# First and last sums of squares of a hybrid decoder block: an early table load, sums by source, single stores

## The chip, the cores and the metric

The kernel runs on one core of one Trainium2 chip. The metric is the device time of one execution in microseconds, and lower is better. The kernel before was timed three times: 1016.0 us in the median, from 1015.67 to 1016.91. Its profile comes from one further execution. The engines are called as the profile calls them: PE (TensorE, matmuls), PEld (its weight loads), DVE (VectorE), ACT (ScalarE), POOL (GpSimd), SP (SyncE, which issues most DMAs).

## The reference, cut to what matters

One decoder layer in float32, with 512 tokens of width 1024: a feed-forward block, a token-mixing block, a second feed-forward block, and a last RMSNorm. Nine vectors made from the condition `c` shift, scale and gate the three blocks.

```
def rmsnorm(x, g):
    y = x * rsqrt(mean(x * x, axis=-1, keepdims=True) + EPS)
    return y * g

cond = silu(c)
sh1, sc1, gt1, ..., sh3, sc3, gt3 = split(cond @ w_ada + b_ada, 9)
u = rmsnorm(h, g_norm_ffn1) * (1 + sc1) + sh1
h = h + 0.5 * gt1 * swiglu(u, w_ffn1_in, w_ffn1_out)
u = rmsnorm(h, g_norm_mix) * (1 + sc2) + sh2
h = h + gt2 * token_mixing(u, ...)
u = rmsnorm(h, g_norm_ffn2) * (1 + sc3) + sh3
h = h + 0.5 * gt3 * swiglu(u, w_ffn2_in, w_ffn2_out)
return rmsnorm(h, g_final)
```

The change touches the sums of squares of the first RMSNorm, those of the last one with the stores behind it, and the helper that also serves the two RMSNorms between.

## The kernel before, in words

**Layout.** The activations are kept transposed: `H[k]`, k = 0 to 7, is 128 features by 512 tokens. Tokens lie along the free axis, so a mean over features is a sum over partitions and over the eight tiles. Squares are taken on ACT, the eight tiles are added up (mostly on DVE, into `acc`), and PE sums over partitions with a matmul against a tile of ones. Half A is tokens 0 to 255, half Bh tokens 256 to 511.

**Matmuls.** A weight is split into a high and a low part (ACT writes `whi`, L298, DVE writes `wlo`, L310), the activations likewise, and each product is three matmuls (`mm3`, L341 to L343). Plain float32 matmuls, such as the sums, the fillers and the spreads, show two records each in the profile.

**The order of the work.** It is written out by hand: each engine runs its instructions in the order in which the Python code issues them, and so does each DMA queue (SP's, and near the end ACT's). No scheduler moves anything. Semaphores are put in where one engine needs another's result or buffer.

**The head (`startup`).** PE first runs five filler matmuls (`warm`, L1411). SP loads `c` (one row), the eight tiles of `H`, then the first tiles of `wada`, small vectors (`vecs`, `cst`) and the first weights (`raw`). ACT waits for `c`, loads the table for Silu and computes silu(c) into row 0 of a zeroed tile (L1431); two matmuls with ones spread that row over all partitions (L1433). DVE and ACT copy the two halves of the result into `cond` (L1435, L1446; ACT's copy stands between the squares of k = 4 and k = 5). ACT squares the eight tiles of `H` as they land (L1448). DVE adds the squares of k = 0, 2, 4, 6 into `acc` and those of k = 1, 3, 5 into `R` (L1450), then `R` into `acc` (L1454); the square of k = 7 stays alone. Between these PE runs fillers on `H[0]` to `H[5]`, twelve in all, and then the sums from two sources, the square of k = 7 and `acc`, four matmuls each (L1440). The sums come out as 128 equal columns, of which ACT reads one per 128 tokens for the square root (L1458). DVE takes the reciprocal (L1463) between the first two products of `ada_do` (L364, rows of `wada` times `cond`), PE spreads it over the partitions with an identity matrix (L1466), and DVE and ACT make the first normalized tile `UH` (L444, L456). With that the stream of main matmuls starts (L1506, L1508, L1510).

**The helper (`stats_t`, L419 to L432).** For one half it sums over partitions with one matmul per 128 tokens and source, each with a single column of ones, so that the result is one column per 128 tokens. The loop runs over tokens outside and over sources inside. It is called five times beside main matmuls (in `out_tail` and `head`, twice each, and for half A in `out_end`) and once at the very end. `spread` (L434) puts the result back over the partitions, two matmuls of 128 columns for a half.

**The tail (`out_end`).** The last weight matrix is applied in steps m = 3 to 7, first for half A, then for half Bh. After each step DVE adds the gated result to `H[m]` (`tail_step`, L493), ACT squares it into a tile `s` (L494), ACT scales `H[m]` by the last norm's weights into `O[m]` (`scaled`, L545), and DVE adds `s` to `acc` (L580). While half Bh is computed, half A is finished: its sums at the middle of m = 4, its spread at the middle of m = 5, then a multiplication by the spread reciprocal (`final`, L549) of tiles 0 to 3 on POOL, which reads an SBUF copy `R`, and of tiles 4 and 5 (after m = 5) and 6 and 7 (after m = 6) on DVE, which reads the bank. SP stores them in pairs. After m = 7 of half Bh come five fillers (L591), the sums from two sources (`acc` and the last `s`), two more fillers, the spread (L437), and the last eight finals: six on DVE, and tiles 1 and 2 on POOL, for which ACT copies the spread bank into `R` (L601). The stores are (0), (1) and (2) on SP's queue and the pairs (3, 4), (5, 6) and the single (7) on ACT's (L552).

Of the kernel before, what the change touches and what calls it, by code (L numbers as in the profile page):

```python
# [11 lines left out]
AF = mybir.ActivationFunctionType  # L12
OP = mybir.AluOpType

P = 128
T = 512
# [120 lines left out]
class Kernel:  # L137
# [281 lines left out]
    def stats_t(self, bank, hs, parts=None, between=None):  # L419


        n = (hs.stop - hs.start) // P
        r, c = self.r4[:, hs.start // P:hs.stop // P], slice(hs.start, hs.start + n)
        parts = parts or (self.acc[:, hs],)
        for i in range(n):
            for j, x in enumerate(parts):
                self.nc.tensor.matmul(bank[:, hs.start + i:hs.start + i + 1], x[:, i * P:i * P + P], self.ones[:, 0:1],
                                      start=j == 0, stop=j == len(parts) - 1)
        self.nc.scalar.activation(r, bank[:, c], AF.Sqrt, bias=self.eps, scale=1.0 / D)
        if between:  # L430
            between()
        self.nc.vector.reciprocal(r, r)  # L432
# [102 lines left out]
    def out_end(self, ms, ksrc, gate):  # L535

        nc = self.nc
        v, g = nc.vector, nc.gpsimd
        tiles = {}
        A, Bh = slice(0, HT), slice(HT, T)  # L540
        rA, rB = self.B[6], self.B[7]
        self.held = self.pos

        def scaled(m, hs):
            nc.scalar.activation(self.O[m][:, hs], self.H[m][:, hs], AF.Copy, scale=self.g(3)[:, m:m + 1])  # L545

        def final(e, m, hs, r):
            o = self.O[m][:, hs]
            e.tensor_tensor(o, o, r[:, hs], op=OP.mult)  # L549

        def store(m0, m1, hs, queue):
            queue.dma_start(self.out[m0 * P:m1 * P, hs].rearrange("(m p) t -> p m t", p=P), self.OO[:, m0:m1, hs])  # L552

        for h, hs in enumerate((A, Bh)):
            for m in ms:
                bank = self.nb()
                if h == 0:
                    tiles[m] = ksrc(m)
                    self.split_hi()
                    if m == ms[0]:  # L560
                        nc.scalar.preload_act_table(AF.Sqrt)
                n = len(tiles[m])
                for i, (hi, lo, uh, ul) in enumerate(tiles[m]):
                    if h and m == ms[1] and i == n // 2:
                        self.stats_t(rA, A)
                    if h and m == ms[2] and i == n // 2:
                        self.spread(rA, A)
                        nc.scalar.activation(self.R[:, A], rA[:, A], AF.Copy)
                        for j in range(4):
                            final(g, j, A, self.R)  # L570
                            if j % 2:
                                store(j - 1, j + 1, A, nc.sync)
                    self.mm3(bank[:, hs], hi, lo, uh[:, hs], ul[:, hs], i == 0, i == n - 1)
                s = self.tp.tile([P, T], F32, name="ut")[:, :HT]
                self.tail_step(m, hs, bank, gate, s)
                if h and m == ms[-1]:
                    break
                scaled(m, hs)
                self.split_lo()
                v.tensor_tensor(self.acc[:, hs], self.acc[:, hs], s, op=OP.add)  # L580
                if h and m in ms[2:4]:
                    j = 4 + 2 * (m - ms[2])
                    for x in (j, j + 1):
                        final(v, x, A, rA)
                    store(j, j + 2, A, nc.sync)

        free = self.nb()

        def warm(n):
            for _ in range(n):  # L590
                nc.tensor.matmul(free[:, :P], self.ones, self.ones, start=True, stop=True)  # L591

        warm(5)
        self.stats_t(rB, Bh, (self.acc[:, Bh], s))
        warm(2)
        scaled(ms[-1], Bh)
        self.spread(rB, Bh)

        final(v, 0, Bh, rB)
        store(0, 1, Bh, nc.sync)  # L600
        nc.scalar.activation(self.R[:, Bh], rB[:, Bh], AF.Copy)  # L601
        final(g, 1, Bh, self.R)
        for j in (3, 4, 5, 6, 7):
            final(v, j, Bh, rB)
            if j == 4:
                store(3, 5, Bh, nc.scalar)
                store(1, 2, Bh, nc.sync)
                final(g, 2, Bh, self.R)
        store(5, 7, Bh, nc.scalar)
        store(2, 3, Bh, nc.sync)  # L610
        store(7, 8, Bh, nc.scalar)

    def head(self, n, banks, table):

# [789 lines left out]
    def startup(self):  # L1404
        nc, a = self.nc, self.a
        v, M = nc.vector, nc.tensor.matmul


        def warm(n, x):
            for _ in range(n):  # L1410
                M(self.B[5][:, :P], self.ones, x[:, :P], start=True, stop=True)  # L1411

        v.memset(self.ones, 1.0)
        warm(5, self.ones)

# [22 lines left out]
        def part(s, first, last):  # L1438
            for n in range(4):
                M(self.B[7][:, n * P:(n + 1) * P], s[:, n * P:(n + 1) * P], self.ones, start=first and n == 0, stop=last,  # L1440
                  skip_group_check=True)

        acc = (self.acc, self.R)
        for k in range(KT):
            if k == 5:
                nc.scalar.activation(self.cond[:, T:], self.B[1], AF.Copy)  # L1446
            s = acc[k] if k < 2 else self.tp.tile([P, T], F32, name="ut")
            nc.scalar.activation(s, self.H[k], AF.Square)  # L1448
            if 1 < k < 7:
                v.tensor_tensor(acc[k % 2], acc[k % 2], s, op=OP.add)  # L1450
            if k < 6:
                warm((1, 1, 2, 2, 3, 3)[k], self.H[k])
            elif k == 6:
                v.tensor_tensor(acc[0], acc[0], acc[1], op=OP.add)  # L1454
            else:
                part(s, True, False)
                part(acc[0], False, True)
        nc.scalar.activation(self.r4, self.B[7][:, ::P], AF.Sqrt, bias=self.eps, scale=1.0 / D)  # L1458
        warm(2, self.H[7])

        g, b1 = self.g(0), self.vecs[:, 8:16]
# [117 lines left out]
```

## Time and profile before

| what | value |
|---|---|
| runs of the kernel before, median (lowest to highest) | 1016.0 us (1015.67 to 1016.91) |
| the profiled execution's own time | 1016.32 us |
| its span, first to last instruction | 1014.5 us |
| PE busy | 1003.8 us, 99% |
| DVE busy | 764.8 us, 75% |
| ACT busy | 442.0 us, 44% |
| POOL busy | 26.1 us, 3% |
| granted TensorE clock, mean | 0.998 |
| DMA | 139.61 MB, mean 138 GB/s |

Times within a profile count from the start of its span; about 1.8 us of an execution's own time lie outside the span. "Idle" in a row is the time its engine stood before it, with the instruction or DMA that ended the wait. The chain of work follows the last instruction back, at each step to what released it. Records of matmuls overlap, so a matmul's cost in a stream is the distance between starts, not its duration.

### The profile page before, as it was taken

Reading aid. Unit: us, or ns where it says so; the run is one execution under the profiler, and the core shown is the slowest. Engines: PE = TensorE matmul, PEld = TensorE weight load, DVE = VectorE, ACT = ScalarE, POOL = GpSimd, SP = SyncE. Lnnn points to the kernel's source line nnn. Section 1 sums busy time; section 2 is a strip of 40 time slices with the busy share of each in tenths; the row PEclk is TensorE's granted clock in tenths of the full one; section 3 lists DMA queues with packets and bytes.
Section 4 is the critical chain, followed back from the end, with each engine's and each line's share of the span. In section 5 each row is a group of like instructions: output and inputs, shape, how many; then the busy total and the mean of one; then the engine's idle time right before and its main releaser. Section 6 shows DMA issues by size and latency. Waiting matters only on the chain.

```text
span 1014.5 us, 15763 instructions
## 1 busy us (share of the span) xinstructions
PE 1003.8 (99%) x6448; PEld 912.2 (90%) x6448; DVE 764.8 (75%) x1120; ACT 442.0 (44%) x674; POOL 26.1 (3%) x30
## 2 busy tenths in 40 slices
PE   8999999999999999999999999999999999999997
PEld 7888999989899999889988888998899899998997
DVE  7989979789796667878448776577787776676754
ACT  5443644525435443334323333454366254352553
POOL 0000000000000000008000000000000000000001
PEclk9999999999999999999999999999999999999999
DMA  9856456455454323222155773421353234241312
GB/s 336 274 197 214 146 163 221 148 175 168 148 182 136 104 77 104 63 63 84 32 198 188 253 265 107 122 63 62 95 176 122 66 105 146 84 146 43 113 33 83
DMA packets 43114, 139.61 MB, mean 138 GB/s; under 512 B 4897, under 2 KB 8225, under 8 KB 43042
## 3 DMA queue, kind: packets, MB, share of 16 engines
q1 hardware_dynamic: 42354, 137.95, 41.8%
q8 instruction: 50, 0.82, 0.3%
q10 hardware_dynamic: 688, 0.66, 0.2%
q14 instruction: 22, 0.18, 0.1%
HBM read 135.82 MB, written 2.77 MB: 137 GB/s over the span
## 4 chain that ended last, share of the span: by engine, by line
PE 93%; DVE 5%; ACT 1%; issue 1%; DMA 0%; DVEq 0%; ACTq 0%
PE bank L341 16%; PE bank L342 16%; PE bank L343 16%; PE bank L723 10%; PE bank L725 10%; PE bank L724 10%; PE bank L1506 1%; PE bank L1510 1%; PE bank L1508 1%; PE bank L1097 1%; PE bank L1276 1%; DVE wlo L310 1%; PE bank L1277 1%; PE bank L1278 1%; PE bank L1045 1%; PE bank L1074 1%
## 5 line engine op out<-in xcount | busy, mean ns | idle before, releaser
L310 DVE TENSOR_TENSOR wlo<-raw,whi 128x1024 fp32r<-128x1024 f32 (+6 forms) x166 | 174.4, 1062 | 66.5 <-ACT whi L298 65.9
L298 ACT ACTIVATE whi<-raw 128x1024 fp32r<-128x1024 f32 (+6 forms) x166 | 150.0, 920 | 47.6 <-DVE raw L242 41.6
L725 PE MATMUL bank<-UH,wlo 128*128 128x256 f32 x544 | 150.5, 277 | 0.0
L723 PE MATMUL bank<-UH,whi 128*128 128x256 f32 x544 | 150.5, 277 | 0.0
L724 PE MATMUL bank<-UL,whi 128*128 128x256 f32 x544 | 150.5, 277 | 0.0
L341 PE MATMUL bank<-HI,whi 128*128 128x512 f32 (+1 forms) x406 | 146.6, 361 | 0.0
L342 PE MATMUL bank<-HK,whi 128*128 128x512 f32 (+1 forms) x406 | 146.4, 361 | 0.0
L343 PE MATMUL bank<-HI,wlo 128*128 128x512 f32 (+1 forms) x406 | 146.2, 360 | 0.0
L341 PE MATMUL bank<-UH,whi 128*128 128x512 f32 (+1 forms) x400 | 145.9, 365 | 0.0
L343 PE MATMUL bank<-UH,wlo 128*128 128x512 f32 (+1 forms) x400 | 141.8, 355 | 0.5 <-DVE wlo L310 0.5
L342 PE MATMUL bank<-UL,whi 128*128 128x512 f32 (+1 forms) x400 | 141.8, 355 | 0.1
L310 DVE TENSOR_TENSOR wlo<-X,whi 128x1024 fp32r<-128x1024 f32 (+4 forms) x106 | 111.7, 1064 | 33.3 <-ACT whi L298 32.9
L298 ACT ACTIVATE whi<-X 128x1024 fp32r<-128x1024 f32 (+4 forms) x106 | 95.7, 927 | 46.3 <-DVE X L242 45.6
L723 PE MATMUL bank<-SH,whi 128*128 128x256 f32 x408 | 113.8, 279 | 0.1
L724 PE MATMUL bank<-SL,whi 128*128 128x256 f32 x408 | 113.6, 278 | 0.0
L725 PE MATMUL bank<-SH,wlo 128*128 128x256 f32 x408 | 113.6, 278 | 0.0
L724 PEld LDWEIGHTS bank<-UL,whi 128*128 128x128 f32 x544 | 102.3, 188 | 0.3
L723 PEld LDWEIGHTS bank<-UH,whi 128*128 128x128 f32 x544 | 102.1, 188 | 0.3
L725 PEld LDWEIGHTS bank<-UH,wlo 128*128 128x128 f32 x544 | 102.1, 188 | 0.0
L342 PEld LDWEIGHTS bank<-HK,whi 128*128 128x128 f32 x406 | 76.3, 188 | 11.8 <-DVE HK L651 0.4
L341 PEld LDWEIGHTS bank<-HI,whi 128*128 128x128 f32 x406 | 76.5, 188 | 11.5
L343 PEld LDWEIGHTS bank<-HI,wlo 128*128 128x128 f32 x406 | 76.4, 188 | 11.6
(228 smaller groups left out, 1760.2 us busy)
## 6 DMA issues: line engine op xcount, KB each, us to landing
ada<-wada SPq DMA_DIRECT2D x47, 512.0 KB, 5.0
raw<-wmix SPq DMA_DIRECT2D x44, 512.0 KB, 3.6
raw<-wf1i SPq DMA_DIRECT2D x32, 512.0 KB, 4.4
raw<-wf2i SPq DMA_DIRECT2D x30, 512.0 KB, 3.6
X<-wf2i SPq DMA_DIRECT2D x14, 512.0 KB, 3.6
cs<-wada SPq DMA_DIRECT2D x12, 512.0 KB, 3.5
AR<-wada SPq DMA_DIRECT2D x12, 512.0 KB, 4.2
raw<-wf2o SPq DMA_DIRECT2D x12, 512.0 KB, 3.6
```

The costliest lines, as they stand in the source:

```text
L298: self.nc.scalar.activation(self.hi[:, y], r[:, x], AF.Copy)
L310: self.nc.vector.tensor_tensor(self.lo[:, y], r[:, x], self.hi[:, y], op=OP.subtract)
L341: M(ps, hi, uh, start=start, stop=False)
L342: M(ps, hi, ul, start=False, stop=False)
L343: M(ps, lo, uh, start=False, stop=stop)
L723: M(o, hi, uh, start=start and p == 0 and k == 0, stop=False, skip_group_check=True)
L724: M(o, hi, ul, start=False, stop=False, skip_group_check=True)
L725: M(o, lo, uh, start=False, stop=k == 3, skip_group_check=True)
L1045: M(S[:, o + i * P:o + i * P + P], qz[:, (2 * i + h) * P:(2 * i + h + 1) * P], k[:, toks], start=True, stop=True)
L1074: nc.tensor.transpose(b[:, i * P:i * P + P], p[:, i * P:i * P + P], self.ident)
L1097: M(o, pt[:, blk * P:blk * P + P], v, start=i == 0, stop=i == len(srcs) - 1)
L1276: M(b, self.UH[k][:, c::4], hi, start=k == 0, stop=False)
```

## The change

In the head, the load of the Silu table is issued at the start of ACT's work, ahead of the wait for `c`. ACT's copy of the second half of `cond` moves behind all eight squares. DVE's addition of the two partial sums is dropped; PE sums three sources instead (`R`, the square of k = 7, `acc`), and three more fillers run, on `H[6]`.

In the helper, each matmul multiplies by the whole tile of ones (128 columns) instead of one column, the loop over sources is the outer one, and ACT reads every 128th column.

In the tail, POOL also does final 6 of half A; DVE does 4, 5 and 7 after m = 5, and the pair (6, 7) is stored after m = 6. The square of m = 6 of half Bh isn't added to `acc`; it is a source of its own. The five fillers are dropped. The last reciprocal is spread twice, into two banks; DVE's finals read the one, ACT's copy for POOL the other. The last eight tiles are stored singly, in turn on SP's queue (0, 4, 1, 7) and ACT's (3, 5, 6, 2).

```diff
--- before.py
+++ after.py
@@ -420,12 +420,12 @@
 
 
         n = (hs.stop - hs.start) // P
-        r, c = self.r4[:, hs.start // P:hs.stop // P], slice(hs.start, hs.start + n)
+        r, c = self.r4[:, hs.start // P:hs.stop // P], slice(hs.start, hs.stop, P)
         parts = parts or (self.acc[:, hs],)
-        for i in range(n):
-            for j, x in enumerate(parts):
-                self.nc.tensor.matmul(bank[:, hs.start + i:hs.start + i + 1], x[:, i * P:i * P + P], self.ones[:, 0:1],
-                                      start=j == 0, stop=j == len(parts) - 1)
+        for j, x in enumerate(parts):
+            for i in range(n):
+                self.nc.tensor.matmul(bank[:, hs.start + i * P:hs.start + i * P + P], x[:, i * P:i * P + P], self.ones,
+                                      start=i == j == 0, stop=j == len(parts) - 1, skip_group_check=True)
         self.nc.scalar.activation(r, bank[:, c], AF.Sqrt, bias=self.eps, scale=1.0 / D)
         if between:
             between()
@@ -566,7 +566,7 @@
                     if h and m == ms[2] and i == n // 2:
                         self.spread(rA, A)
                         nc.scalar.activation(self.R[:, A], rA[:, A], AF.Copy)
-                        for j in range(4):
+                        for j in (0, 1, 2, 3, 6):
                             final(g, j, A, self.R)
                             if j % 2:
                                 store(j - 1, j + 1, A, nc.sync)
@@ -577,12 +577,15 @@
                     break
                 scaled(m, hs)
                 self.split_lo()
+                if h and m == ms[-2]:
+                    s6 = s
+                    store(6, 8, A, nc.sync)
+                    continue
                 v.tensor_tensor(self.acc[:, hs], self.acc[:, hs], s, op=OP.add)
-                if h and m in ms[2:4]:
-                    j = 4 + 2 * (m - ms[2])
-                    for x in (j, j + 1):
+                if h and m == ms[2]:
+                    for x in (4, 5, 7):
                         final(v, x, A, rA)
-                    store(j, j + 2, A, nc.sync)
+                    store(4, 6, A, nc.sync)
 
         free = self.nb()
 
@@ -590,25 +593,18 @@
             for _ in range(n):
                 nc.tensor.matmul(free[:, :P], self.ones, self.ones, start=True, stop=True)
 
-        warm(5)
-        self.stats_t(rB, Bh, (self.acc[:, Bh], s))
+        self.stats_t(rB, Bh, (self.acc[:, Bh], s6, s))
         warm(2)
         scaled(ms[-1], Bh)
         self.spread(rB, Bh)
 
-        final(v, 0, Bh, rB)
-        store(0, 1, Bh, nc.sync)
-        nc.scalar.activation(self.R[:, Bh], rB[:, Bh], AF.Copy)
-        final(g, 1, Bh, self.R)
-        for j in (3, 4, 5, 6, 7):
-            final(v, j, Bh, rB)
-            if j == 4:
-                store(3, 5, Bh, nc.scalar)
-                store(1, 2, Bh, nc.sync)
-                final(g, 2, Bh, self.R)
-        store(5, 7, Bh, nc.scalar)
-        store(2, 3, Bh, nc.sync)
-        store(7, 8, Bh, nc.scalar)
+        rC = self.nb()
+        self.spread(rC, Bh)
+        nc.scalar.activation(self.R[:, Bh], rC[:, Bh], AF.Copy)
+        for e, j, queue in ((v, 0, nc.sync), (v, 3, nc.scalar), (v, 4, nc.sync), (v, 5, nc.scalar), (g, 1, nc.sync),
+                            (v, 6, nc.scalar), (v, 7, nc.sync), (g, 2, nc.scalar)):
+            final(e, j, Bh, self.R if e is g else rB)
+            store(j, j + 1, Bh, queue)
 
     def head(self, n, banks, table):
 
@@ -1410,6 +1406,7 @@
             for _ in range(n):
                 M(self.B[5][:, :P], self.ones, x[:, :P], start=True, stop=True)
 
+        nc.scalar.preload_act_table(AF.Silu)
         v.memset(self.ones, 1.0)
         warm(5, self.ones)
 
@@ -1442,19 +1439,17 @@
 
         acc = (self.acc, self.R)
         for k in range(KT):
-            if k == 5:
-                nc.scalar.activation(self.cond[:, T:], self.B[1], AF.Copy)
             s = acc[k] if k < 2 else self.tp.tile([P, T], F32, name="ut")
             nc.scalar.activation(s, self.H[k], AF.Square)
             if 1 < k < 7:
                 v.tensor_tensor(acc[k % 2], acc[k % 2], s, op=OP.add)
-            if k < 6:
-                warm((1, 1, 2, 2, 3, 3)[k], self.H[k])
-            elif k == 6:
-                v.tensor_tensor(acc[0], acc[0], acc[1], op=OP.add)
-            else:
-                part(s, True, False)
-                part(acc[0], False, True)
+            if k < 7:
+                warm((1, 1, 2, 2, 3, 3, 3)[k], self.H[k])
+            if k == 6:
+                part(acc[1], True, False)
+        nc.scalar.activation(self.cond[:, T:], self.B[1], AF.Copy)
+        part(s, False, False)
+        part(acc[0], False, True)
         nc.scalar.activation(self.r4, self.B[7][:, ::P], AF.Sqrt, bias=self.eps, scale=1.0 / D)
         warm(2, self.H[7])
```

## The prediction, made before the changed kernel ran

> **What bounds the kernel now.** I read the page first: PE is busy for 99% of the span and the chain that ended last is 93% PE, so the stream of matmuls from 16.9 us to 1004.1 us sets the time and the change leaves it alone. What is left is the head before that stream and the tail behind it. So I read the chain of work in these two windows, then PE's timeline record by record, then the landing times of the DMAs.
>
> The head, chain of 0 to 30 us (start, length, what):
>
> ```profile
> 2.20 1.28 ACT L1431
> 3.49 1.06 ACT X L1431
> ...
> 4.60 3.78 PE bank L1433 x4
> 8.38 3.41 PE bank L1411 x24
> 11.79 1.80 PE bank L1440 x16
> ...
> 13.62 0.27 ACT r L1458
> ...
> 16.90 2.11 PE bank L1506 x8
> ```
>
> c lands at 2.13, the table load (1.28) stands behind it, then Silu, the two matmuls that spread it, twelve filler matmuls (L1411, two records each) and the sums. PE's timeline shows two rates for one form:
>
> ```profile
> 8.18 0.85 PE L1411 MATMUL bank<-H,ones 128*128 128x128 f32 x3
> 11.07 0.61 PE L1411 MATMUL bank<-H,ones 128*128 128x128 f32 x4
> ```
>
> Starts are 0.213 us apart until 9.7 and 0.111 from 9.85 on (the clock row reads 1.00 in both, so only the spacing shows it). PE worked from 1.05 to 3.55, stood for 1.05 us, and worked without a gap from 4.60: the fast rate came 5.2 us after the last gap.
>
> The tail, chain of 999.5 us to the end:
>
> ```profile
> 1004.01 0.66 DVE out L549 x2
> 1004.67 0.41 DVE H L493
> ...
> 1005.16 0.42 ACT ut L494
> ...
> 1005.63 0.83 PE bank L427 x6
> 1006.46 0.55 PE bank L591 x4
> 1007.01 0.72 PE bank L437 x4
> ...
> 1007.76 0.43 DVE out L549
> ...
> 1008.21 0.39 ACT AR L601
> ...
> 1008.63 0.42 DVE out L549
> ```
>
> The last matmul record of the stream starts at 1003.86 and ends at 1004.14, but H's last step waits for DVE's two finals. Later DVE's first final, ACT's copy of the same bank and DVE's second final go one behind the other. Then DMA: bytes move at 335 to 351 GB/s from 1010.4 to 1012.8; the last store (issued 1010.60, 2.9 us) lands at 1013.5.
>
> **Head.** ACT's load needs nothing, so it runs from about 0.8 to 2.1 and Silu starts at 2.2: X is ready 1.28 earlier, at 3.26, and PE starts the spread at 3.31. Its five opening matmuls stream until 3.19, so the gap of 1.05 shrinks to about 0.1. Counted from 1.05, the same 5.2 us put the fast rate at 6.3. The spread's four records (1.02, 0.85, 0.85, 0.86 apart) would end at 6.9; what is left at 6.3 halves: 6.6.
>
> PE's work grows: 15 fillers instead of 12, 12 sum matmuls instead of 8. A matmul is two records, 0.222 us fast and 0.427 slow. The fillers wait for H: H3 to H6 land at 7.3, 7.9, 8.5 and 9.2 (issue plus landing), so the last three end at 9.2 + 0.67 = 9.9. The 12 sums take 2.67; with 0.17 for the last one's end ACT's Sqrt starts at 12.7 instead of 13.62. Their sources are there in time: the squares, bound by H's landing, end at about 10.4 (10.63 before), the odd sum is done at 9.95, the even one at 10.6. DVE's joining add (0.69) goes.
>
> DVE is next. c's second half is now copied by ACT behind the squares, 10.4 to 11.0 (8.48 before); ada's first tile lands at 4.86 + 6.3 = 11.16, so the later copy costs nothing as long as the squares end by 10.5, and each 0.1 us beyond that costs 0.1. DVE starts ada at 11.2 (11.56 before) and reaches the reciprocal 1.84 later, 13.04 instead of 13.91. The stream's first matmul moves by the same 0.87, to 16.03.
>
> It can't keep all of that. ada's third tile (1) lands between raw 0 (14.4) and ada 9 (16.9); 512 KB at 410 GB/s is 1.28 us, so about 15.65, where DVE wants it at 15.1. DVE's later work therefore moves by only 0.36: UH of k = 1 is ready at 21.82 (22.18), PE wants it at 21.6 and starts at 21.86 instead of 22.47. Later steps of DVE lie 5.32 apart, PE's 5.44, so no more is lost. **Head: -0.6.** Bounds: -0.87 if that tile lands early; +1.0 if the fast rate still comes at 9.8, for then PE has spread and fillers at 0.427 until 9.8, and the added matmuls put Sqrt at 14.6.
>
> The Trainium skill's page "TensorE: Matmul & The Clock Gate", Part 1, has the clock rise at the end of a fully busy window of about 3.4 us that runs free of the kernel. By that rule the windows of this execution end at 6.4 and 9.8, the first spoiled by the gap: my sum hardly changes, but in another execution the rise could lie as late as 1.05 + 6.8 = 7.9, by which the estimate of the head would be about 0.1 instead of -0.6. One trace can't show the phase.
>
> **Middle.** stats_t has five calls beside main matmuls; each of its two matmuls now streams 128 columns of ones instead of one. The window around the last call, and around a spread of the new shape (128 columns, two matmuls):
>
> ```profile
> 995.72 0.28 PE L343 MATMUL bank<-HI,wlo 128*128 128x256 f32 x1
> 995.84 0.50 PE L427 MATMUL bank<-ones,AR 128*128 128x1 f32 x4
> ...
> 996.41 0.28 PE L342 MATMUL bank<-HK,whi 128*128 128x256 f32 x1
> ```
>
> ```profile
> 998.29 0.28 PE L343 MATMUL bank<-HI,wlo 128*128 128x256 f32 x1
> 998.41 0.61 PE L437 MATMUL bank<-cst,r 128*128 128x128 f32 x4
> ...
> 998.98 0.28 PE L342 MATMUL bank<-HK,whi 128*128 128x256 f32 x1
> ```
>
> From the record before to the second one behind: 0.69 in both. The weight loads (0.19 each, four) set the pace, not the columns. I take **0**; the chain (0.34 against 0.44) gives the other end, +0.1 a call, +0.5.
>
> **Tail.** At m = 5 DVE does three finals instead of two (+0.33), so H of m = 6 starts at 2.9 instead of 2.57 (all in us from 1000) and its square is done at 3.85. Then DVE has nothing: the add (0.43) and two finals (0.66) of m = 6 are gone. H of m = 7 starts when PE is done, 4.16 instead of 4.67; DVE is idle from 3.4, 0.75 us of cover. POOL's fifth final (0.74) ends at 3.3, and its store's 256 KB are out before the last ones begin. PE meanwhile sums acc and the square of m = 6 (eight records, until about 4.9), in place of the five fillers. The last square is ready at 4.16 + 0.48 + 0.08 + 0.46 = 5.18; two matmuls follow instead of three. By the spread's 0.72 for four records behind a wait, Sqrt starts at 5.94 instead of 6.50: -0.56.
>
> From there to DVE's first final nothing changes: 7.20. The second spread follows on PE (four records, 0.44), so ACT's copy starts at 7.65 and POOL's two finals end at about 9.5 (10.09 before). DVE no longer waits for the copy; its six finals are done at 7.62, 7.95, 8.28, 8.61, 8.94 and 9.27, where the last ended at 10.38. Stores are issued at 7.66 (0), 8.05 (3, ACT behind its copy), 8.32, 8.65, 8.9, 9.1, 9.32 and 9.55 (2); an issue costs 0.34 on SP, 0.45 on ACT, which two queues in turn absorb. A lone 128 KB store took 1.7: about 0.87 until its bytes move, 0.39 of moving at 340 GB/s, 0.45 until it landed (estimates from slices of 0.4 us). The eight keep the engines full from 8.53: 8 x 0.385 = 3.08, so 11.61, landed at 12.06 instead of 13.5. **Tail: -1.45.** Bounds: -0.56, if the drain behind the chain keeps its length; -2.25, if only the last store's own 1.7 counts (9.55 + 1.7 = 11.25).
>
> **Sum.** -0.6 + 0 - 1.45 = -2.05. The profiled execution took 1016.32 (span 1014.5): 1014.27. The median of the runs is 0.32 lower, which would give 1013.95. I say **1014.1**. About 0.2% (2.03 us) is what a measurement of this kernel can tell from no change, so the forecast lies on that line.
>
> **Rivals.**
> 1. *The clock doesn't come early.* The fast rate stays near 9.8, PE's added work is slow and PE becomes the bound of the head: +1.0 - 1.45 = -0.45, 1015.7. For it: one observation of the rise. Against: the gap before it is gone.
> 2. *The drain is no shorter.* The last bytes follow the chain alone: -0.6 - 0.56, 1015.1. For it: engines already full from 10.4. Against: bytes start over a microsecond earlier.
> 3. *Single stores wait for one another*, the case that ends slower. Place: the two queues at the end. If each of four stores on a queue took its lone 1.7 before the next begins, ACT's would land at 8.05 + 6.8 = 14.85, +1.35; with the head's -0.6 that is +0.75, 1017.0. It decides from (13.5 - 8.05) / 4 = 1.36 us a store without overlap. Against: ACT's stores issued at 10.08 and 10.60 landed 0.3 apart. The Trainium skill, "DMA: Bandwidth & Descriptors", Rules for kernel authors, advises joining small transfers; that speaks for this rival.
> 4. *The change doesn't do what it says*: ACT's copy still waits for DVE. The built order of instructions has it wait for PE alone on another bank; DVE's finals wait for no copy. No chance kept.
>
> **How the numbers follow.** Forecast 0.65 (own range 1013.0 to 1015.0), rival 1 0.17, rival 2 0.14, rival 3 0.04. Two thirds of the forecast's own share lies below 1013.97: faster by over 0.2% 0.43, within 0.2% 0.53, slower 0.04. The range 1013.0 to 1015.8 takes in rivals 1 and 2.
>
> **What would show it.** Silu at 2.2, PE without a gap from 1.05, spacing 0.111 from about 6.4, Sqrt at 12.7, the stream's first matmul at 16.0 and its second step at 21.9. A stats_t call still 0.69 wide. H of m = 7 right behind PE; six finals of DVE in a row; last store landed 1.4 us sooner behind the stream's end. A spacing of 0.213 beyond 8 us, or bytes at under 330 GB/s at the end, would make it wrong.

## The result and the profile after

The changed kernel took **1014.68 us** in the median of 22 runs (1014.05 to 1015.5); the kernel before took 1016.0 in 22 runs beside them (1015.32 to 1017.45). The ratio is 0.9986, 95% interval 0.998 to 0.9992: 1.3 us faster. The interval excludes 1, and the gain is less than the 0.2% that the forecast took as its line. The profiled execution took 1014.89, its span is 1013.1: 1.43 and 1.4 less than before.

**Head.** The chain of work of the changed kernel up to 20 us (start, length, what); its lines of fillers, sums and main matmuls carry new line numbers:

```profile
2.02 4.42 DMA H<-xT
6.44 0.04 issue
6.49 3.61 PE bank L1407 x26
10.09 2.80 PE bank L1437 x24
...
12.91 0.27 ACT r L1453
...
13.21 0.19 DVE r L1458
...
16.20 2.14 PE bank L1501 x8
```

The table load is gone from it and H's transfer stands at its head. Sqrt starts at 12.91 (13.62 before), the stream at 16.20 (16.90). PE's timeline of the same execution (start, length, line, number):

```profile
1.05 2.50 PE L1407 MATMUL bank<-ones 128*128 128x128 f32 x10 [1.05 <-DVE ones L1410]
3.35 2.61 PE L1430 MATMUL bank<-X,ones 128*128 128x512 f32 x4
5.79 4.30 PE L1407 MATMUL bank<-H,ones 128*128 128x128 f32 x30
```

No row but the first has an idle time: the gap of 1.05 us is closed. The spread's four records take 2.61 instead of 3.78, because the distance between starts falls to its fast value within them, at about 4.7 us; the thirty filler records behind are fast. At 0.111 each they would take 3.3 us; the rest of their 4.30 is mostly waiting for H's tiles.

**Tail.** The chain of the changed kernel is followed back from POOL and loses itself there, so the timelines of PE, DVE and ACT are read instead:

```profile
1003.83 0.28 PE L343 MATMUL bank<-HI,wlo 128*128 128x256 f32 x1
...
1005.20 0.71 PE L427 MATMUL bank<-ones,ut 128*128 128x128 f32 x4 [0.20 <-ACT ut L494]
...
1006.46 1.16 PE L437 MATMUL bank<-cst,r 128*128 128x128 f32 x8
```

```profile
1004.15 0.48 DVE L493 SCALAR_TENSOR_TENSOR H<-bank,mod,H 128x256 f32<-128x256 f32 x1 [0.79 <-PE bank L343]
...
1007.21 2.08 DVE L549 TENSOR_TENSOR out<-out,bank 128x256 f32<-128x256 f32 x6 [0.80 <-PE bank L437]
```

```profile
1005.94 0.26 ACT L429 ACTIVATE r<-bank,eps 128x2 f32<-128x2 f32 x1 [0.80 <-PE bank L427]
...
1007.66 0.38 ACT L603 ACTIVATE AR<-bank 128x256 f32<-128x256 f32 x1 [1.05 <-PE bank L437]
```

DVE has waited 0.79 us for PE when H's last step starts (two finals were ahead of it before), the six finals are one row without a break, and ACT's copy begins while they run. The bytes of this end, in slices of 0.275 us from 1003 to 1014 us (GB/s):

```profile
GB/s 0 26 328 335 343 331 361 343 354 343 97 0 0 0 0 0 0 0 0 0 309 320 339 346 339 343 343 335 347 339 343 112 0 0 0 0 0 0 0 0
```

The second block is the eight single stores: full from the first slice on, 3.1 us long. The kernel before, in slices of 0.4 us from 1000 to 1016 us:

```profile
GB/s 0 0 0 0 23 346 287 0 44 325 361 353 228 13 328 310 5 0 0 0 0 0 105 223 0 79 343 335 338 341 351 336 172 0 0 0 0 0 0 0
```

There the engines run dry behind the first store (0, 79) before the rest of the block.

**Middle.** Around the last call of `stats_t` beside main matmuls:

```profile
995.70 0.28 PE L343 MATMUL bank<-HI,wlo 128*128 128x256 f32 x1
995.82 0.61 PE L427 MATMUL bank<-ones,AR 128*128 128x128 f32 x4
...
996.38 0.28 PE L342 MATMUL bank<-HK,whi 128*128 128x256 f32 x1
```

From the record before to the second behind: 0.68; it was 0.69 with one column.

### The profile page after: what moved, and what is told of

The parts are those of the page before. It is cut to its first block, busy times and chain, and to the rows that moved or that the text cites. A ratio compares the mean times of both kernels' runs of the same rounds, so it can differ in the third digit from the quotient of the medians.

```text
span 1013.1 us, 15788 instructions
## 1 busy us (share of the span) xinstructions
PE 1004.4 (99%) x6460; PEld 912.8 (90%) x6460; DVE 763.9 (75%) x1117; ACT 442.8 (44%) x674; POOL 26.9 (3%) x31
## 4 chain that ended last, share of the span: by engine, by line
PE 87%; DVE 7%; issue 2%; DMA 2%; ACT 1%; POOL 0%; SPq 0%; POOLq 0%; DVEq 0%; ACTq 0%
PE bank L342 15%; PE bank L343 15%; PE bank L341 15%; PE bank L719 10%; PE bank L721 10%; PE bank L720 10%; DVE wlo L310 2%; PE bank L1501 1%; PE bank L1503 1%; PE bank L1505 1%; PE bank L1093 1%; PE bank L1272 1%; DVE H L864 1%; PE bank L1273 1%; PE bank L1274 1%
```

## The experiments

**Theory:** the tail gives the whole measured gain, 1.3 to 1.4 us; the head's 0.5 is real early in the stream (its third step) and gone at its end. **Rival:** head and tail each give a part that lasts. A second question is which part of the tail and of the head does it.

### The head alone

The new `startup` with the old tail and the old helper.

> The head of the change alone (early table load, three sums, fifteen fillers; helper and tail as before). Theory: the head starts the stream 0.7 us sooner (first L1506 at 16.2 instead of 16.9, second step about 0.5 sooner), but at about 117 us DVE waits for a load of ffn weights whose landing does not move with the stream, so that what is left at the end of the stream is anything from 0 to 0.5 us from execution to execution: median 0.1 to 0.5 below before. Rival 1: the whole 0.5 to 0.6 stays in every execution and the profile of the changed kernel was an unlucky one: median 0.5 to 0.6 below. Rival 2: the load is the bound whenever the stream is early: median 0.0 to 0.1 below, and every profile shows the stall near 120 us.

1015.91 against 1015.94 in the same job, ratio 1.0 (0.9991 to 1.0009). No gain is seen in the time, and 0.9 us either way isn't excluded. In the profile the first main matmul started 0.41 sooner than before (16.49), the third step 0.19 sooner, and these 0.19 were still there at the last main matmul (1003.67 for 1003.86). By the median (0.03 below) it is rival 2's case, but rival 2 asked for a stall near 120 us in every profile, and this one has none.

### The tail and the helper alone

The old `startup` with the new `out_end` and `stats_t`.

> The tail and the helper of the change alone (head as before). Theory: the end of the stream stays where it was and the tail gives 1.4 us: span 1.4 below before, median 1014.6. If the two parts simply add, the head alone and the tail alone together give the change's 1.3 to 1.4 within the noise. Rival: the helper's 128 columns cost up to 0.1 a call, so that the tail alone gives only 0.9 and the head has paid the rest.

1014.71 against 1015.94, ratio 0.9989 (0.998 to 0.9997): 1.23 faster, nearly as much as the whole change. The medians of the two runs fit the theory, but with 0.9 us open either way they don't exclude a part of 0.4 from the head.

### The gap closed by fillers instead of the load

```diff
-        warm(5, self.ones)
+        warm(8, self.ones)
```

The kernel before, with three more opening fillers.

> The kernel before with eight opening fillers instead of five and nothing else changed: PE works from 1.05 to about 4.4, nearly up to the spread at 4.60, so the gap of 1.05 us is closed without moving the table load. Theory (the fast rate comes after an unbroken stretch of work): the record spacing of the fillers on H falls to 0.111 between 4.5 and 8 us instead of 9.85, ACT's Sqrt starts at about 12.7 to 13.0 instead of 13.62, and the stream starts 0.6 to 0.9 sooner, as early as with the whole head of the change. Rival: the early table load makes the gain, and the gap has nothing to do with the rate: spacing 0.213 until 9.8, Sqrt at 13.6, nothing moves.

1015.75, ratio 0.9995 (0.9987 to 1.0004), no gain that can be told. But the matmuls' distance fell to the fast value at about 5.5 us instead of 9.85 (the first two of the spread's four records lie 0.91 apart, the next 0.43), Sqrt came at 12.96 and the stream started at 16.37, 0.53 sooner. It is the gap, not the table load, that held the fast rate back.

### The changed kernel again

> The changed kernel again, for a second profile. Theory (the load's landing near 117 us varies by itself): the offset of the stream against before after 121 us differs from the 0.0 of the first profile, somewhere between 0 and -0.5. Rival (the load is the bound when the stream is early): again 0.0, with DVE waiting 2.4 us for the load and PE 0.2 us behind it. The moment at which the filler spacing falls to 0.111 (4.7 in the first profile) also tells whether it moves from one execution to the next.

1014.76. With the same instructions the fast rate came at about 6.3 us instead of 4.7, H[6] landed at 9.80 instead of 9.11, and Sqrt started at 13.60 instead of 12.91. Single executions differ in the head by as much as the edit is worth. After 121 us this stream stood 0.20 behind the kernel before: neither 0 to 0.5 ahead of it, as the theory had it, nor level with it after a wait of 2.4 us, as the rival had it (DVE waited 1.85 for the load and PE lost nothing there).

### No second bank

```diff
-        rC = self.nb()
-        self.spread(rC, Bh)
-        nc.scalar.activation(self.R[:, Bh], rC[:, Bh], AF.Copy)
+        nc.scalar.activation(self.R[:, Bh], rB[:, Bh], AF.Copy)
```

> The changed kernel without the second spread: ACT's copy for POOL reads the same bank as DVE's finals and stands ahead of them. Theory (the end is the time at which the first bytes move plus 3.1 us of moving): the copy starts at 7.2 instead of 7.66 (us from 1000, against the end of the stream as in the first profile), DVE's first final at 7.64 instead of 7.21, so the last store lands 0.4 later and the median is 0.4 above the changed kernel. Rival (the last of POOL's finals sets the end): POOL starts 0.45 sooner, its last store too, and the kernel is up to 0.4 faster than the changed one.

1014.69 (11 runs), not to be told from the change by its time. The tail shows it, DVE's timeline of this kernel:

```profile
1008.14 2.07 DVE L549 TENSOR_TENSOR out<-out,bank 128x256 f32<-128x256 f32 x6 [1.22 <-ACT AR L601]
```

DVE waits 1.22 us, the last part of it for ACT's copy of the same bank (0.80, for PE alone, with two banks). Counted from the last main matmul, the first final moves from 3.38 to 3.79 and the last store's landing from 8.25 to 8.65: the second bank is worth 0.4, against this order, in which ACT's copy stands ahead of all six finals (in the kernel before, one final was ahead of it).

### The stores grouped as before

```diff
-            store(j, j + 1, Bh, queue)
+            if j in (4, 6):
+                store(j - 1, j + 1, Bh, nc.scalar)
+            elif j not in (3, 5):
+                store(j, j + 1, Bh, nc.scalar if j == 7 else nc.sync)
```

> The changed kernel with the last half tiles stored as before: (0), (1), (2) on SP's queue, the pairs (3, 4) and (5, 6) and the single (7) on ACT's. Everything up to the last finals is the same. Theory (bytes move at 340 GB/s from the first store on and two stores in flight share them): the pairs delay the bytes of 3 and 5 by 0.33 each and leave one gap behind store 0, so the end is 0.2 to 0.5 later. Rival (single stores pay a fixed part each): pairs end sooner or at the same time.

1015.06 (11 runs), ratio 0.9989 (0.998 to 0.9998). The bytes at its end, same slices:

```profile
GB/s 149 0 0 194 320 372 302 372 339 350 346 261 4 0 0 0 0 0 0 0 0 141 313 22 231 324 354 350 324 354 354 332 350 321 45 0 0 0 0 0
```

Behind the first store (141, 313) the engines run dry (22): the next one waits for its second tile. The last landing that the trace holds is 8.59 behind the last main matmul, 0.34 later than with single ones (the landing of store (2) is missing; the span ends 0.38 later by the same count). The dry slice and its two neighbours fall short of a full rate by about as much (0.37 us at 340 GB/s, an estimate): single stores are worth 0.34 because the second one starts sooner.

### No opening fillers

```diff
-        warm(5, self.ones)
```

The changed kernel without the first five fillers (one run).

> The changed kernel without the five opening fillers, so that PE's work begins with the spread of c at 3.3. Theory (the fast rate comes at the end of a window of about 3.4 us that is full of work, and the windows stand anywhere): spacing falls to 0.111 between 6.7 and 10.2 us instead of 4.6 to 7.9; each us beyond about 7 delays the sums by 0.5, so ACT's Sqrt starts between 12.9 and 14.6. Rival (the early load alone makes the head): Sqrt at 12.9 to 13.6 as in the two profiles of the changed kernel, whatever the spacing.

1014.94. PE's first work is the spread at 3.39, the fast rate comes at about 7.75, and Sqrt 4.26 us behind H[6]'s landing instead of 3.80. Sqrt's time, 13.60, lies where theory and rival overlap; the distance to H[6] tells them apart, since Sqrt came 3.80 to 3.83 behind H[6] in the three profiles of the changed kernel.

### H taken out of the head's way

H[4] to H[7] are loaded behind the second weights, and the sums square H[0] to H[3] twice, so that the kernel leaves out half of the first sum (one run).

> The changed kernel with half of H taken out of the head: H4 to H7 are loaded behind the second weights, and the first sums square H0 to H3 twice (so the first normalization uses another sum; the amount of work is the same). Theory (the landing of H bounds the head of the changed kernel, not PE or ACT): fillers and sums no longer wait, Sqrt starts at about 11.5 to 12.0 instead of 12.9 to 13.6, and DVE's first product of ada, which waits for its tile, starts 2 us or more sooner than 11.2. Rival (PE's 15 fillers and 12 sums bound the head): Sqrt stays within 0.5 of 12.9.

1014.44. The fillers never waited, and yet Sqrt started at 13.26:

```profile
7.01 3.53 PE L1407 MATMUL bank<-H,ones 128*128 128x128 f32 x30
10.38 1.06 PE L1439 MATMUL bank<-ones,AR 128*128 128x128 f32 x8
11.27 1.06 PE L1439 MATMUL bank<-ones,ut 128*128 128x128 f32 x8
12.16 1.06 PE L1439 MATMUL bank<-ones,AR 128*128 128x128 f32 x8
```

PE's rows run back to back from 7.0 on. The fast rate came only at 7.0 in this execution, so 15 fillers and 12 sums were themselves the bound: the theory's early Sqrt was missed. DVE's first product of `ada` started at 10.05, 1.2 sooner and not 2, since its own sums lasted until 9.99.

### Three fillers fewer, and a first store cut in two

```diff
-            if k < 7:
-                warm((1, 1, 2, 2, 3, 3, 3)[k], self.H[k])
+            if k < 6:
+                warm((1, 1, 2, 2, 3, 3)[k], self.H[k])
...
-            final(e, j, Bh, self.R if e is g else rB)
-            store(j, j + 1, Bh, queue)
+            for x in (slice(HT, HT + P), slice(HT + P, T)) if j == 0 else (Bh,):
+                final(e, j, x, self.R if e is g else rB)
+                store(j, j + 1, x, queue)
```

> The changed kernel without the three fillers on H[6], and with the first of the last eight tiles finished and stored in two halves of 128 tokens. Head: in five profiles with three sums Sqrt started 3.80 us after H[6] landed. Theory (PE's own work sets Sqrt): 0.5 to 0.67 less, so 3.1 to 3.3; the first main matmul gains only 0.15, since DVE's two ada products (1.84 from their start) are then the last. Rival (H[7]'s square sets it): still 3.8. Tail: theory (the drain at 340 GB/s runs on without a break from the first byte): the first store is issued 0.2 earlier, and the last lands 8.05 us behind the last main matmul's start instead of 8.25. Rival (the end follows the last finals): 8.35, since DVE's six finals take 0.1 longer. Time: 0.2 to 0.4 below the changed kernel by the theories, or the same.

1014.65. Both theories fell. Sqrt still comes 3.80 behind H[6], and PE's row says why:

```profile
9.95 1.16 PE L1438 MATMUL bank<-ones,AR 128*128 128x128 f32 x8 [0.51 <-DVE AR L1446]
```

The fillers left, and the sums start at the same time: they wait for DVE's odd sum, done at 9.90. In the changed kernel the two ends coincide (9.93 and 9.88). At the end the last store lands at 8.43 instead of 8.25: after the first half store the engines ran dry again (224, 56, 304 GB/s in three slices), as with pairs; the added final also puts the last stores 0.07 to 0.10 later.

### The early load alone, with the old sums

```diff
+        nc.scalar.preload_act_table(AF.Silu)
         v.memset(self.ones, 1.0)
```

On the kernel with the old head and the new tail.

> The early table load alone in the head, with the old two sums, the joining addition and ACT's copy in its old place; new helper and tail. Theory (the three sums and three more fillers make Sqrt wait for PE, and the early load alone would do as well): Sqrt at H[6]'s landing plus 4.1 or less, the distance from the first main matmul to that at 28 us as in before, median as the changed kernel's, 1014.7 within 0.3. Rival (the three sums are what makes the head shorter): first main matmul at 16.9 as before, 1015.0 or more.

1014.58, ratio 0.9984 (0.9975 to 0.9993). Sqrt comes 3.89 behind H[6], 0.09 later than with three sums. The stream started at 16.02, so the rival is out. From the first main matmul to the third step it took 11.50 and not 11.01 as in the kernel before: that part of the theory was missed. The three sums and the dropped joining addition are worth next to nothing.

### Eight fillers with the new tail, and the change once more

> The head of before with eight opening fillers instead of five (which fill PE's gap), and the whole new helper and tail. Theory (the tail gives all of the change; what a head gains depends on when H lands and is mostly lost at the loads of the first weights): median within 0.3 us of the changed kernel in this job, about 1014.6; in the trace the last store lands 8.25 us behind the last main matmul's start, as in the changed kernel. Rival (the old sums behind a closed gap are the better head and the gain lasts): 0.5 us below the changed kernel, about 1014.1, with the distance between the first main matmul and the one at 28 us no longer than before, 0.15 to 0.45 us shorter than with three sums.

> The changed kernel again, for direct comparison on the same chip: 1014.7, with the last store 8.25 us behind the last main matmul's start, and Sqrt 3.8 us behind H[6]'s landing wherever that falls.

Run in one job, with 33 runs of the kernel before at 1016.29: 1014.28 (1013.73 to 1015.18; ratio 0.9982, 0.9973 to 0.9991) with eight fillers, and 1014.89 (1014.03 to 1016.11; 0.9984, 0.9976 to 0.9993) for the changed kernel. The lowest median of the study belongs to the old head with three more fillers, 0.61 below the changed kernel beside it. That is more than the theory's 0.3 and near the rival's number, but the rival's sign is missing: from the first main matmul to the third step it took 11.24, and 11.20 with three sums. The intervals overlap: no version is shown to beat the changed one.

### All profiles side by side

Starts in us. "wada" is the landing of the first tile of `wada`; "first" and "third" are the main matmuls that begin the stream's first and third step (16.90 and 27.91 in the kernel before), counted from it. "28 to 360" is what the stream lost between those times against the kernel before, and "end" the last store's landing, counted from the last main matmul's start.

| kernel | wada | first | third | 28 to 360 | end |
|---|---|---|---|---|---|
| before | 11.20 | 5.70 | 16.71 | 0 | 9.61 |
| tail alone (old head) | 11.26 | 5.79 | 16.81 | 0.46 | 8.23 |
| eight fillers, old tail | 10.82 | 5.55 | 16.56 | 0.20 | 9.59 |
| no opening fillers | 11.36 | 5.52 | 16.57 | 0.75 | 8.25 |
| changed | 11.12 | 5.08 | 16.28 | 0.53 | 8.25 |
| changed, second | 11.81 | 5.08 | 16.29 | 0.40 | 8.25 |
| changed, third | 10.94 | 5.08 | 16.29 | 0.84 | 8.24 |
| head alone | 11.43 | 5.06 | 16.29 | 0.03 | 9.59 |
| no second bank | 11.99 | 5.07 | 16.32 | 0.80 | 8.65 |
| grouped stores | 11.82 | 4.85 | 16.31 | 0.30 | 8.59 |
| eight fillers, new tail | 11.52 | 5.04 | 16.28 | 0.19 | 8.24 |
| fewer fillers, cut store | 11.18 | 5.04 | 16.23 | 0.50 | 8.43 |
| early load alone | 11.25 | 4.77 | 16.27 | 0.05 | 8.24 |

Two columns are sharp to a few hundredths. The end depends on the tail's code alone. The third step comes 16.23 to 16.32 behind the landing of the first `wada` tile in nine of the thirteen, whether they have the early load or eight fillers, three sums or two: there transfers set the pace. In exactly these nine DVE's product with ada's third tile waits for that tile to land, 0.19 to 0.50 us. In the changed kernel:

```profile
15.58 1.23 DVE L364 SCALAR_TENSOR_TENSOR ada<-ada,cond 128x1024 f32<-128x1024 f32 x1 [0.19 <-DMA ada<-wada]
```

The old head was 0.4 to 0.5 above that floor. Above it are the two with the gap, the one without opening fillers (a late fast rate in all three), and eight fillers with the old tail, where `wada` landed earliest and DVE, at the joining addition until 11.63, began its products 0.81 behind it (0.10 in the changed kernel). The other two columns are scatter. The landing itself lies between 10.82 and 11.99 for the same loads, and up to 0.84 is lost between 28 and 360 us, with old heads and new.

The loss doesn't grow with the lead. The five profiles with the earliest third step (27.23 to 27.52 us) lost 0.42 in the mean, the five with the latest (27.93 to 28.31) 0.54. So nothing here shows that an early stream is held up more than a late one. Most of these differences in time come from when the loads landed; that a lead made by code lasts as well is argued, not shown.

One more difference has no cause in the code. From 366 to 382 us, PE's busy time with its number of matmuls, the other engines, the granted clock, DMA share and GB/s, of the kernel before and of the second run of the changed one:

```profile
366.00:382.00 16.00, 16.00 (x138) 16.00 (x137) 9.31 (x19) 5.18 (x9) 0.00 (x0) 1.00 0.22 67
```

```profile
366.00:382.00 16.00, 16.00 (x144) 16.00 (x143) 9.71 (x20) 5.76 (x10) 0.00 (x0) 1.00 0.21 67
```

Without any wait, six matmuls more pass at the same clock row: 0.113 us apart instead of 0.118. Eight of the fourteen profiles have the one and six the other, the three of the changed kernel among both; it is worth 0.6 us.

## Why the prediction was right, and where it was wrong

The forecast was 1014.1, the median is 1014.68, inside the range of 1013.0 to 1015.8. The profiled execution moved by -1.43 where the sum said -2.05.

- **Tail, forecast -1.45: right.** In one execution: H's last step 1004.15 (1004.16 forecast), Sqrt 1005.94 (1005.94), first final 1007.21 (1007.20), last store landed 1012.08 (12.06). The landing moved by 1.36 against the stream. Of this the chain gives 0.53 by the two profiles (Sqrt 2.11 instead of 2.64 behind the last main matmul; no run has it alone), the second bank 0.40 and single stores 0.34 by the runs without them, together 1.27. The split is rough: a run that takes one part out prices it in the changed order, not in the old one.
- **Middle, forecast 0: right.** 0.68 for 0.69, and the stream keeps its distance to the kernel before from 122 to 1003 us between -0.03 and 0.05.
- **Head, forecast -0.6: nearly right at the third step, gone at the end of this execution.** Sqrt came at 12.91 instead of 12.7 and the first main matmul at 16.20 instead of 16.03; -0.65 at the second step (-0.61 forecast), -0.51 at the third. The step that failed is *"Later steps of DVE lie 5.32 apart, PE's 5.44, so no more is lost"*. It looked at DVE against PE and not at later transfers. DVE's rows for the loads that it splits at 117 us, before and after:

```profile
117.25 1.23 DVE L242 TENSOR_TENSOR X<-X,raw 128x1024 f32<-128x1024 f32 x1 [1.49 <-DMA X<-wf1i]
```

```profile
117.72 1.23 DVE L242 TENSOR_TENSOR X<-X,raw 128x1024 f32<-128x1024 f32 x1 [2.38 <-DMA X<-wf1i]
```

  The load was issued 0.42 earlier (111.88 for 112.30) and landed 0.47 later (117.60 for 117.13): it took 5.72 instead of 4.83. ACT's split of it came late by as much, and behind that split stands ACT's `u` (L726), for which PE then stood 0.22 us at 120.57. Its lead of 0.48 at 119.5 was 0.02 behind at 121.5. But this is a late transfer, not a price of the lead: with the tail alone, whose stream ran 0.15 behind the kernel before, the same load also took 5.72 and the stream lost 0.45 there. In the fourteen profiles the load took 4.29 to 5.72. In the others such a loss falls at this load, near 236 us, or hardly at all. That the lead was gone in the profile is partly the luck of this pair of executions: the kernel before met no late load here, and the head alone kept its 0.19 to the end. Its time gave 0.0 with an interval of 0.9 either way, so whether the 0.4 lasts on average stays open.
- **The reason given for the fast rate failed, its direction held.** "5.2 us after the last gap" would be 6.3. With PE at work from 1.05 without a break the fast rate came at about 4.7, 6.3 and 4.4 in three profiles of the same kernel, as early as 4.2 without the second bank and as late as 7.0 with H out of the way; with the gap left in, at 9.85 and 10.0. It did no harm that the time was missed: Sqrt came 3.80 to 3.83 behind H[6] with the rise at 4.7, 6.3 and 4.4. The Trainium skill, "TensorE: Matmul & The Clock Gate", Part 1, has a window of some 3.4 us that runs free of the kernel and must be busy throughout. By that rule the rise lies, as an estimate, 3.4 to 6.8 us after unbroken work begins. These runs agree but for 0.25 us at the lower end: 3.15 to 5.95 after 1.05.
- **Rivals.** The first and second are out: the fast rate came early, the drain was shorter. What happened to the time of the profiled execution, a late transfer in the stream, was on no list. The third, single stores that wait for one another, is out too: the last two of ACT's four landed at 11.32 and 12.08, 0.76 apart and not 1.36 or more, and the first at 9.80 (the trace lacks the landing of the second). The Trainium skill, "DMA: Bandwidth & Descriptors", Rules for kernel authors, would join small transfers; here joining costs 0.34 where it delays the second store (the trace disagrees for 128 KB at this place), and a store cut to 64 KB costs 0.18, again with dry engines behind it.

## What to carry to other kernels

At the end of a kernel, count from the last matmul of the stream: those distances repeat to 0.02 us when whole times scatter by 1 us, and one profile then tells what each edit is worth. The end is set by when the first store's bytes start and whether the engines then stay full, so free the first result and issue the second store before the first has drained. A lead won at the start of a long stream can be hidden, in a comparison of two executions, by one transfer that lands late; look for DVE or ACT rows that wait for a DMA, and compare several profiles before counting it as kept or lost.

## What the runs showed of the hardware that was not expected

- The same loads of H and `wada` at the same issue times land up to 1.2 us apart from one execution to the next (10.82 to 11.99 for the first `wada` tile).
- Matmuls without waits ran 0.113 or 0.118 us apart in the same 16 us, at the same granted clock of 1.00.
- A float32 matmul with 128 columns of ones cost as much as one with a single column: 0.68 and 0.69 for two of them in the stream.
